# A prefix state through normed x, three token tiles, pre-tiled weights and a placed schedule, in a two-layer mLSTM and gMLP trunk on eight cores

## The chip, the cores and the metric

The kernel runs on all 8 cores of one Trainium2 chip: cores 0 to 3 are die 0, cores 4 to 7 are die 1. The metric is the device time of the slowest core, in microseconds. Each number of a profile below is of one execution, read on its slowest core.

The granted TensorE clock below is the share of its full clock that TensorE was allowed, as the profile records it. An execution of this program falls into one of two states. In the fast state all eight cores agree within about 1%. In the slow state the cores of one die (sometimes both) show a lower granted TensorE clock and the time is some per cent longer, whatever the kernel. Only fast runs are compared here, with fast runs. A ratio is the mean time of one kernel's fast runs over that of the kernel before's fast runs of the same rounds. So it is not quite the ratio of the medians that are quoted beside it.

## The reference

Input and output are (4 batches, 4096 tokens, 2048 channels) in f32. There are two layers, each with an RMS norm in front and a residual add behind, and a final norm. Cut to what matters:

```python
def mlstm_layer(xn, ...):                 # layer 0
    p = xn @ w_in                         # columns [q | k | v | o | z | gates]
    qk = silu(causal_depthwise_conv(p[..., :o1], conv_w, conv_b))   # 4 taps
    ...                                   # 8 heads: q, k 256 wide; v 512 wide
    hc = mlstm_cell(q * 256 ** -0.5, k, v, ig, lf)
    hc = hc * sigmoid(o); hc = hc * rsqrt(mean(hc * hc) + EPS) * head_g
    return (hc * silu(z)) @ w_out

def _mlstm_chunk(carry, inp):             # the cell, chunk by chunk
    ...
    h = num / max(|den|, exp(-m_t))
    c_new = decay * c_st + einsum('bhsd,bhse->bhde', k * wexp, v)   # state: 256 x 512 a head
    n_new = decay * n_st + einsum('bhs,bhsd->bhd', wexp, k)

def gmlp_layer(xn, ...):                  # layer 1
    p = xn @ w_in                         # [u | v | z], u and v through gelu
    sv = einsum('gts,bcsgd->bctgd', tril(w_s), layernorm(v)) + b_s   # within 128 tokens
    return (u * sv * silu(z)) @ w_out
```

## The kernel before

Core c takes batch c // 2 and half c % 2 of its tokens, 2048 of them. The second half of a sequence needs the cell's state at the end of the first half. So every core first computes that state from the first half's tokens (the "prefix") and multiplies it by a flag of 0 or 1. After that it runs both layers on its own tokens ("main"). Matmuls are bf16 with 512 columns at most. A weight tile is 2048 x 512, 2 MB as bf16; GpSimd's queue loads it and converts it from f32, into three slots in turn.

The prefix takes the 2048 tokens as four tiles of 512. For every head it projects k and v and updates the state once a chunk of 128 tokens:

```python
def state_update(h, c, cbi):
    for cc in range(2):
        tk.mm([lambda p, cc=cc: p.matmul(PK[cc][:, :], lhsT=kp[:, c, cc * 128:(cc + 1) * 128], rhs=vt[:, c, :],
                                         start=True, stop=True)], ...)
    ...
    for cc in range(2):
        tk.op("dve", lambda v, cc=cc: v.tensor_tensor(out=Cst[:, h, cc, :], in0=PK[cc][:, :], in1=Cst[:, h, cc, :],
                                                      op=ALU.add), ...)
    ...
    for cc in range(2):
        tk.op("act", lambda a, cc=cc: a.activation(out=Cst[:, h, cc, :], in_=Cst[:, h, cc, :], func=AF.Copy, scale=eg), ...)
```

Main takes four tiles of 512 tokens too. Each starts with a barrier and with the norm of its own x, which needs the x load, which needs the buffer of the previous tile's residual:

```python
for t in range(NT):
    tk.barrier()
    layer0(t)
    layer1(t)
    final_norm(t)          # ends with: ensure_gain(g0bc_d); load_x(xm, t + 1)
```

Weights are read from the original matrices, so a partition's share of a tile comes as 16 pieces of 2 KB in f32:

```python
w_in0v = w_in0.rearrange("(kc p) c -> p kc c", p=128)
def col_tile(wv, c0, n=512):
    return [(0, n, 0, KC, wv[:, :, c0:c0 + n])]
```

The softmax here doesn't subtract the row's maximum and nothing guards it: scores larger than these inputs give would overflow.

Of the kernel before, what the change touches and what calls it, by code (L numbers as in the profile page):

```python
# [6 lines left out]
F32 = mybir.dt.float32  # L7
BF16 = mybir.dt.bfloat16
AF = mybir.ActivationFunctionType
ALU = mybir.AluOpType  # L10

D = 2048
NTOK = 2048
T = 512
NSUB = T // 128
NT = NTOK // T
KC = D // 128
H = 8
EPS = 1e-6
IN0 = 16400  # L20
IN1 = 12288
SAME_ENGINE_SYNC = True
NWSLOT = 3

class Buf:
    __slots__ = ("w", "r", "name")

    def __init__(self, name=""):
        self.w = None
        self.r = {}  # L30
        self.name = name

# [5 lines left out]

class TK:
    def __init__(self, nc, es):  # L40
        self.nc = nc
        self.es = es
        self.eng = {"pe": nc.tensor, "act": nc.scalar, "dve": nc.vector,
                    "pool": nc.gpsimd, "sp": nc.sync}
        self.sem = {k: es.enter_context(nc.semaphore("s_" + k)) for k in self.eng}
        self.cnt = {k: 0 for k in self.eng}
        self.seen = {k: {} for k in self.eng}
        self.ndsem = 0

    def dsem(self):  # L50
        self.ndsem += 1
        key = "d%d" % self.ndsem
        return DSem(self.es.enter_context(self.nc.semaphore(key)), key)

    def wait(self, e, tk):
        if tk is None:
            return
        sem, val, key = tk
        if key == e and (e == "pe" or not SAME_ENGINE_SYNC):
            return  # L60
        if self.seen[e].get(key, 0) >= val:
            return
        self.eng[e].wait_ge(sem, val)
        self.seen[e][key] = val

    def _deps(self, e, reads, writes):
        for b in reads:
            self.wait(e, b.w)
        for b in writes:
            self.wait(e, b.w)  # L70
            for t in b.r.values():
                self.wait(e, t)
# [8 lines left out]
    def op(self, e, fn, reads=(), writes=()):  # L81
        self._deps(e, reads, writes)
# [4 lines left out]
        self._mark(tk, reads, writes)  # L87
        return tk

    def mm(self, fns, reads=(), writes=()):  # L90
        e = "pe"
        self._deps(e, reads, writes)
        ins = None
        for fn in fns:
            ins = fn(self.eng[e])
        self.cnt[e] += 1
        ins.then_inc(self.sem[e], 1)
        tk = (self.sem[e], self.cnt[e], e)
        self._mark(tk, reads, writes)
        return tk  # L100

    def dma(self, e, ds, out, in_, reads=(), writes=()):
        self._deps(e, reads, writes)
# [3 lines left out]
        self._mark(tk, reads, writes)  # L107
        return tk

    def snapshot(self):  # L110
        return [(self.sem[e], self.cnt[e], e) for e in ("pe", "act", "dve") if self.cnt[e] > 0]

    def barrier(self, engines=("pe", "act", "dve", "sp"), tks=None):
        if tks is None:
            tks = self.snapshot()
        for f in engines:
            for tk in tks:
                if tk[2] != f:
                    self.wait(f, tk)

class WQ:
    def __init__(self, tk, slots, tiles):
        self.tk = tk
        self.slots = slots
        self.tiles = tiles
        self.nl = 0
        self.nu = 0

    def _load(self):
        i = self.nl  # L130
        if i >= len(self.tiles):
            return
        t, b, ds = self.slots[i % len(self.slots)]
        tk = self.tk
        tk._deps("pool", (), [b])
        for (co, ncol, k0, nk, src) in self.tiles[i]:
            tk.eng["pool"].dma_start(out=t[:, k0:k0 + nk, co:co + ncol], in_=src).then_inc(ds.sem, 16)  # L137
            ds.cnt += 16
        tk._mark((ds.sem, ds.cnt, ds.key), (), [b])
        self.nl += 1  # L140

    def prime(self):
        for _ in self.slots:
            self._load()

    def cur(self):
        assert self.nu < len(self.tiles), "weight stream exhausted"
        t, b, ds = self.slots[self.nu % len(self.slots)]
        return t, b

    def peek(self, k):
        assert self.nu + k < self.nl, "tile not prefetched yet"
        t, b, ds = self.slots[(self.nu + k) % len(self.slots)]
        return t, b

    def done(self):
        self.nu += 1
        self._load()

def build_program():  # L160
    nc = bass.Bass("TRN2", target_bir_lowering=False)
    dt = lambda n, s, k="ExternalInput": nc.dram_tensor(n, s, F32, kind=k).ap()
    xm = dt("xm", [NTOK, D])
    xp = dt("xp", [NTOK, D])
    flag_d = dt("flag", [128, 1])
    w_in0 = dt("w_in0", [D, IN0])
    w_out0 = dt("w_out0", [4096, D])
    w_in1 = dt("w_in1", [D, IN1])
    w_out1 = dt("w_out1", [4096, D])
    g0bc_d = dt("g0bc", [128, D])  # L170
    g1bc_d = dt("g1bc", [128, D])
    gfbc_d = dt("gfbc", [128, D])
# [3 lines left out]
    hgbc_d = dt("hgbc", [128, 4096])  # L176
# [3 lines left out]
    bsbc_d = dt("bsbc", [128, 8 * 128])  # L180
# [3 lines left out]

    w_in0v = w_in0.rearrange("(kc p) c -> p kc c", p=128)
    w_in1v = w_in1.rearrange("(kc p) c -> p kc c", p=128)
    w_out0v = w_out0.rearrange("(kc p) c -> p kc c", p=128)
    w_out1v = w_out1.rearrange("(kc p) c -> p kc c", p=128)

    with ExitStack() as es:  # L190
        tk = TK(nc, es)
        sb = lambda n, s, d: es.enter_context(nc.sbuf_tensor("sb_" + n, s, d))
        ps = lambda n, s, d: es.enter_context(nc.psum_tensor("ps_" + n, s, d))

        Hs = sb("Hs", [128, NSUB, D], F32)
        Hb = [Buf("H%d" % i) for i in range(NSUB)]
        xnT = sb("xnT", [128, KC, T], BF16)
        xnTb = [Buf("xnT%d" % i) for i in range(NSUB)]
        YT = sb("YT", [128, 32, T], BF16)
        YTb = [Buf("YT%d" % i) for i in range(32)]  # L200
        Cst = sb("Cst", [128, H, 2, 512], F32)
        Cstb = [[Buf("C%d_%d" % (i, j)) for j in range(2)] for i in range(H)]
        nst = sb("nst", [128, H, 2], F32)
        nstb = [Buf("n%d" % i) for i in range(H)]
        wslots = []
        for i in range(NWSLOT):
            wslots.append((sb("w%d" % i, [128, KC, 512], BF16), Buf("w%d" % i), tk.dsem()))
        AB = sb("AB", [128, 12544], BF16)
        AFt = sb("AFt", [128, 1540], F32)
        xnb = AB[:, 6144:8192]  # L210
        xnbb = Buf("xnb")
        wg = sb("wg", [128, KC, 16], BF16); wgb = Buf()
        flag = sb("flagt", [128, 1], F32); flagb = Buf()
        convw = sb("convw", [128, 32, 4], F32); convwb = Buf()
        convb = sb("convb", [128, 32], F32); convbb = Buf()
        gateb = sb("gateb", [128, 16], F32); gatebb = Buf()
        lng = sb("lng", [128, 32], F32); lngb = Buf()
        lnb = sb("lnb", [128, 32], F32); lnbb = Buf()
        wsf = AFt[:, 0:1024].rearrange("p (g t) -> p g t", g=8); wsfb = Buf()
        wsm = sb("wsm", [128, 8, 128], BF16); wsmb = Buf()  # L220
        bsbc = sb("bsbc", [128, 8, 128], F32); bsbcb = Buf()
        rsbc = sb("rsbc", [128, 8, 128], F32); rsbcb = Buf()
        maskT = sb("maskT", [128, 128], F32); maskTb = Buf()
        identf = AFt[:, 1028:1156]; identfb = Buf()
        ident = sb("ident", [128, 128], BF16); identb = Buf()
        onesf = sb("onesf", [128, 128], F32); onesfb = Buf()
        onesb = sb("onesb", [128, 2], BF16); onesbb = Buf()
        hgh1 = sb("hgh", [128, 512], F32)
        hgh = [hgh1, hgh1]
        hghb1 = Buf()  # L230
        hghb = [hghb1, hghb1]
        hghs1 = tk.dsem()
        hghs = [hghs1, hghs1]
        halo = sb("halo", [128, 32, 4], F32); halob = [Buf() for _ in range(32)]
        gI = sb("gI", [128, NSUB, 8], F32); gIb = Buf()
        gZ = sb("gZ", [128, NSUB, 8], F32); gZb = Buf()
        gA = sb("gA", [128, NSUB, 8], F32); gAb = Buf()
        gL = sb("gL", [128, NSUB, 8], F32); gLb = Buf()
        beta = sb("beta", [128, NSUB, 8], F32); betab = Buf()
        beta16 = sb("beta16", [128, NSUB, 8], F32); beta16b = Buf()  # L240
        emb = sb("emb", [128, NSUB, 8], F32); embb = Buf()
        egt = sb("egt", [128, NSUB, 8], F32); egb = Buf()
        eg16t = sb("eg16t", [128, NSUB, 8], F32)
        sm = sb("sm", [128, 64], F32)
# [8 lines left out]
        def ab(o, n):  # L253
            return AB[:, o:o + n]
# [713 lines left out]
```

## Time and profile before

| reading | value | view |
|---|---|---|
| time, 3 runs | 5990, 6005 and 6534 us, the last slow | run times |
| TensorE busy | 5260.5 of 6024.2 us, 87% | page, part 1 |
| end of the prefix | 1190 us, TensorE busy 944 | stretches |
| rest | 4834 us, TensorE busy 4317 | stretches |
| TensorE idle at the start of a main tile | 45.5 to 47.9 us, three times | waits of those stretches |

The page of the kernel before, parts 1 to 4. Part 1 is busy time, its share and the number of instructions. Part 2 cuts the span into 40 slices, in tenths of busy time or of full clock. Part 3 is the DMA queues with packets, MB and their share of the 16 engines' time. Part 4 is the chain of work that ended last, by engine.

```profile
span 6024.2 us, 74749 instructions; the slowest of 8 cores (5953.9 to 6024.2 us)
PE 5260.5 (87%) x26660; PEld 2447.1 (41%) x26660; DVE 1937.1 (32%) x3333; ACT 2254.9 (37%) x4580; POOL 448.9 (7%) x397
...
PE   4988878788899996888899968888999778889998
...
PEclk8878887899999998999999989999999889999999
...
DMA packets 826206, 790.53 MB, mean 131 GB/s; under 512 B 10608, under 2 KB 813808, under 8 KB 818160
...
q0 software_dynamic: 811152, 713.12, 90.9%
...
PE 78%; DVE 7%; ACT 6%; issue 5%; DMA 3%; DVEq 0%; SPq 0%; ACTq 0%; another core or an unknown queue 0%; POOLq 0%
```

TensorE is the engine to look at: nothing else is half as busy, and it makes up 78% of the chain. The PE row dips to 6 or 7 at slices 16, 24 and 32, eight slices apart. Those are the starts of the second to fourth main tile.

The same kernel's stretches: the prefix and the rest. Columns are the stretch, its length, the busy time of each engine (with instructions), the granted clock, the DMA share and GB/s.

```profile
0.00:1190.20 1190.20, 943.60 (x4821) 435.37 (x4822) 431.86 (x722) 521.70 (x1069) 89.36 (x82) 0.84 0.94 118
1190.20:6024.20 4834.00, 4316.95 (x21845) 2011.78 (x21842) 1505.29 (x2611) 1733.25 (x3511) 359.51 (x315) 0.97 0.95 135
```

Its waits of TensorE. Each line says who waited (engine, tile, line), for whom, us in total, times and the longest.

```profile
PE ps_PT L422 <- DVE sb_AB L411: 154.3, 7, 47.9
PE ps_PS L694 <- DVE sb_sm L716: 136.8, 96, 1.8
PE ps_PT L739 <- DVE sb_AB L753: 101.6, 64, 2.1
PE ps_PT L422 <- ACT sb_AB L396: 46.9, 1, 46.9
...
PE ps_PJ L443 <- DMA sb_w<-w_in: 4.0, 1, 4.0
PE ps_PJ L457 <- DMA sb_w<-w_out: 3.0, 2, 1.8
```

A wait of 47.9 us once is another thing than 96 waits of 1.8 us: the first is a hole, the second a chain that is a little too long for its slot. Weight DMA, with 91% of the engines' time on its queue, costs TensorE 8 us in all (4.0 + 3.0 and a line of 1.0 left out). So weights, busy as their queue was, were no limit here.

The hole itself, in the timeline of the kernel before at the start of its second main tile. Columns are start, length, engine, instruction, count, and in brackets the engine's idle time before and what ended it.

```profile
2332.09 7.07 PE L457 MATMUL ps_PS<-sb_w,sb_YT 128*128 128x512 bf16 x32
...
2360.11 6.95 SPq L104 DMA_DIRECT2D sb_Hs<-xm  x4
...
2381.54 1.91 ACT L396 ACTIVATE sb_AB<-sb_Hs 128x2048 bf16<-128x2048 f32 x1 [21.63 <-DMA sb_Hs<-xm]
...
2387.07 1.01 PE L422 MATMUL ps_PT<-sb_ident,sb_AB 128*128 128x128 bf16 x8 [47.91 <-DVE sb_AB L411]
```

The last matmul of one tile ends at 2339.2 us. The final norm then runs, x is asked for at 2360, arrives 21 us later, is squared, scaled and transposed, and TensorE starts again at 2387.

The floor under all this, the time that the matmuls alone would take, is read from one piece of the chain of the kernel before, in order of time (start, length, what):

```profile
1894.98 103.60 PE ps_PJ L452 x480
```

480 matmuls of 512 columns back to back took 103.60 us, 215.8 ns each. The Trainium skill, "TensorE: Matmul & The Clock Gate", section "Wait — 56ns, not 53.3ns?", gives columns / 2.4 ns plus about 2.5 ns, so 215.8; the trace agrees.

### The profile page before, as it was taken

The page shows a single profiled execution, that of the slowest core. Times are in us where ns is not written, and L with a number is a line of the kernel's source. Part 1 is how long each engine was busy: PE and PEld are TensorE (multiplying, and loading weights), DVE is VectorE, ACT ScalarE, POOL GpSimd, SP SyncE. Part 2 cuts the span into 40 slices and gives each one's busy share as a digit, 9 for nine tenths or more (in the row PEclk, how much of TensorE's full clock was granted, in tenths as well). Part 3 has the DMA queues.
Part 4 walks back from the last instruction along what each step waited for, and adds up shares of the span by engine and source line. Part 5 has one row for each costly group of instructions (what it writes and reads, how often), then busy time and mean ns, then how long its engine had stood idle before and what let it go on. Part 6 is the DMA issues. An engine that isn't in the chain of part 4 may idle for free.

```text
span 6024.2 us, 74749 instructions; the slowest of 8 cores (5953.9 to 6024.2 us)
## 1 busy us (share of the span) xinstructions
PE 5260.5 (87%) x26660; PEld 2447.1 (41%) x26660; DVE 1937.1 (32%) x3333; ACT 2254.9 (37%) x4580; POOL 448.9 (7%) x397
## 2 busy tenths in 40 slices
PE   4988878788899996888899968888999778889998
PEld 2434433334444443344444433444444334444443
DVE  2334332333331331334312313333124133341132
ACT  3445443454532321444423214544132045541320
POOL 0000000000000000000000000000000000000000
PEclk8878887899999998999999989999999889999999
DMA  8989899989999999799999996988999979999997
GB/s 137 106 115 119 113 135 108 108 104 120 123 136 143 150 148 162 101 121 125 127 146 150 150 165 102 125 120 127 147 150 151 145 126 122 121 125 146 151 150 127
DMA packets 826206, 790.53 MB, mean 131 GB/s; under 512 B 10608, under 2 KB 813808, under 8 KB 818160
## 3 DMA queue, kind: packets, MB, share of 16 engines
q0 software_dynamic: 811152, 713.12, 90.9%
q1 hardware_dynamic: 14688, 72.61, 3.6%
q8 instruction: 219, 3.59, 0.2%
q14 instruction: 147, 1.20, 0.1%
HBM read 1482.02 MB, written 16.78 MB: 249 GB/s over the span
## 4 chain that ended last, share of the span: by engine, by line
PE 78%; DVE 7%; ACT 6%; issue 5%; DMA 3%; DVEq 0%; SPq 0%; ACTq 0%; another core or an unknown queue 0%; POOLq 0%
PE ps_PJ L452 32%; PE ps_PJ L443 25%; PE ps_PJ L457 7%; PE ps_PS L457 4%; PE ps_PN L457 4%; DVE sb_Cst L544 2%; DVE sb_AFt L516 2%; PE ps_PK L535 1%; DMA sb_Hs<-xm 1%; DVE sb_AB L753 1%; ACT L729 1%; ACT L747 1%; ACT sb_AB L747 1%; ACT sb_AB L396 1%; DMA sb_w<-w_out 1%
## 5 line engine op out<-in xcount | busy, mean ns | idle before, releaser
L452 PE MATMUL ps_PJ<-sb_w,sb_xnT 128*128 128x512 bf16 x9984 | 2292.4, 387 | 60.9 <-ACT sb_AFt L506 25.0
L443 PE MATMUL ps_PJ<-sb_xnT,sb_w 128*128 128x512 bf16 (+1 forms) x7424 | 1645.0, 380 | 19.9 <-ACT sb_AFt L508 14.5
L452 PEld LDWEIGHTS ps_PJ<-sb_w,sb_xnT 128*128 128x128 bf16 x9984 | 974.9, 99 | 1218.0 <-issue 225.5
L443 PEld LDWEIGHTS ps_PJ<-sb_xnT,sb_w 128*128 128x128 bf16 x7424 | 711.3, 100 | 869.3 <-issue 136.8
L137 POOL DMA_DIRECT2D sb_w<-w_in x328 | 374.3, 1142 | 4641.8 <-PE ps_PJ L443 1325.3
L544 DVE TENSOR_TENSOR sb_Cst<-ps_PK,sb_Cst 128x512 f32<-128x512 f32 x512 | 330.8, 687 | 827.8 <-PE ps_PK L535 492.4
L457 PE MATMUL ps_PJ<-sb_w,sb_YT 128*128 128x512 bf16 x2048 | 451.6, 379 | 3.0 <-DMA sb_w<-w_out 3.0
L516 DVE SCALAR_TENSOR_TENSOR sb_AFt<-sb_AFt,sb_convw 128x512 f32<-128x512 f32 x576 | 432.6, 751 | 61.2 <-DVE sb_AFt L516 0.9
L557 ACT ACTIVATE sb_Cst<-sb_Cst,sb_egt 128x512 f32<-128x512 f32 x512 | 340.1, 711 | 69.0 <-DVE sb_Cst L544 63.0
L520 ACT ACTIVATE sb_AB<-sb_AFt 128x512 bf16<-128x512 f32 x192 | 120.8, 629 | 543.5 <-DVE sb_AFt L516 419.2
L457 PEld LDWEIGHTS ps_PJ<-sb_w,sb_YT 128*128 128x128 bf16 x2048 | 199.8, 98 | 243.5 <-issue 4.4
L396 ACT ACTIVATE sb_AB<-sb_Hs 128x2048 bf16<-128x2048 f32 x48 | 91.3, 1902 | 529.4 <-DVE sb_sm L391 439.2
L512 DVE TENSOR_SCALAR sb_AFt<-sb_AFt,sb_convw,sb_convb 128x512 f32<-128x512 f32 x192 | 105.3, 549 | 562.4 <-ACT sb_AFt L508 562.4
L858 DVE SCALAR_TENSOR_TENSOR sb_AFt<-ps_PD,sb_lng,sb_bsbc 128x512 f32<-128x512 f32 x128 | 96.1, 750 | 466.4 <-PE ps_PD L855 466.3
L535 PE MATMUL ps_PK<-sb_AB 128*128 128x512 bf16 x512 | 177.5, 407 | 68.3 <-DVE sb_Cst L544 42.7
L422 PE MATMUL ps_PT<-sb_ident,sb_AB 128*128 128x128 bf16 x192 | 19.5, 263 | 241.3 <-DVE sb_AB L411 154.3
L457 PE MATMUL ps_PN<-sb_w,sb_YT 128*128 128x512 bf16 x1024 | 230.2, 379 | 0.0
L457 PE MATMUL ps_PS<-sb_w,sb_YT 128*128 128x512 bf16 x1024 | 230.2, 379 | 0.0
L769 DVE TENSOR_TENSOR sb_Hs<-ps_PJ,sb_Hs 128x512 f32<-128x512 f32 x64 | 44.2, 691 | 563.0 <-PE ps_PJ L457 563.0
L882 ACT ACTIVATE sb_AB<-sb_Hs 128x2048 bf16<-128x2048 f32 x16 | 30.5, 1909 | 446.7 <-DVE sb_sm L880 445.6
L508 ACT ACTIVATE sb_AFt<-ps_PJ 128x512 f32<-128x512 f32 x192 | 114.6, 597 | 198.8 <-PE ps_PJ L443 187.1
L694 PE MATMUL ps_PS<-sb_AB 128*128 128x128 bf16 x256 | 35.7, 222 | 158.6 <-DVE sb_sm L716 136.8
(152 smaller groups left out, 3918.9 us busy)
## 6 DMA issues: line engine op xcount, KB each, us to landing
sb_w<-w_in POOLq DMA_DIRECT2D x224, 2048.0 KB, 18.5
sb_w<-w_out POOLq DMA_DIRECT2D x64, 2048.0 KB, 16.1
sb_w<-w_in POOLq DMA_DIRECT2D x104, 1024.0 KB, 18.7
sb_Hs<-xp SPq DMA_DIRECT2D x16, 1024.0 KB, 6.9
sb_Hs<-xm SPq DMA_DIRECT2D x16, 1024.0 KB, 22.7
out<-sb_YT SPq DMA_DIRECT2D x16, 1024.0 KB, 29.3
sb_hgh<-hgbc SPq DMA_DIRECT2D x32, 256.0 KB, 4.3
sb_AB<-g0bc SPq DMA_DIRECT2D x4, 1024.0 KB, 16.5
```

The costliest lines, as they stand in the source:

```text
L137: tk.eng["pool"].dma_start(out=t[:, k0:k0 + nk, co:co + ncol], in_=src).then_inc(ds.sem, 16)
L396: tk.op("act", lambda a: a.activation(out=junkN, in_=Hs[:, s, :], func=AF.Square, accum_out=sm[:, s:s + 1]), reads=[Hb[s]], writes=[junkNb ...
L443: tk.mm([lambda p, kc=kc: p.matmul(pj[:, 0:n], lhsT=wt[:, kc, c0:c0 + 128], rhs=xnT[:, kc, t0:t0 + n], start=(kc == 0), stop=(kc == KC - 1 ...
L452: fns = [lambda p, kc=kc: p.matmul(pj[:, 0:n], lhsT=xnT[:, kc, s * 128:(s + 1) * 128], rhs=wt[:, kc, 0:n], start=(start and kc == 0), stop ...
L457: fns = [lambda p, kc=kc: p.matmul(pj[:, 0:n], lhsT=lhs(kc), rhs=wt[:, kc, 0:n], start=(start and kc == 0), stop=(stop and kc == kcs - 1)) ...
L508: tk.op("act", lambda a: a.activation(out=cbuf[:, 3:3 + T], in_=pj[:, 0:T], func=AF.Copy), reads=[pjb], writes=[cbufb])
L516: tk.op("dve", lambda v, j=j: v.scalar_tensor_tensor(out=acc, in0=cbuf[:, j:j + T], scalar=convw[:, ch, j:j + 1], in1=acc, op0=ALU.mult, o ...
L520: tk.op("act", lambda a: a.activation(out=dstT[:, cc, :], in_=acc, func=AF.Silu), reads=[accb], writes=[dstb])
L535: tk.mm([lambda p, cc=cc: p.matmul(PK[cc][:, :], lhsT=kp[:, c, cc * 128:(cc + 1) * 128], rhs=vt[:, c, :], start=True, stop=True)], reads=[ ...
L544: tk.op("dve", lambda v, cc=cc: v.tensor_tensor(out=Cst[:, h, cc, :], in0=PK[cc][:, :], in1=Cst[:, h, cc, :], op=ALU.add), reads=[PKb[cc]] ...
L557: tk.op("act", lambda a, cc=cc: a.activation(out=Cst[:, h, cc, :], in_=Cst[:, h, cc, :], func=AF.Copy, scale=eg), reads=[egb], writes=[Cst ...
L747: tk.op("act", lambda a, c=c, pj=pj: a.activation(out=sz[:, c, :], in_=pj[:, :], func=AF.Silu), reads=[pjb], writes=[szb])
```

## The change

The intent has five parts.

1. Prefix state in another order. With v = xn Wv, the state at the end of the prefix is the sum over tokens of w k v, which equals (sum over tokens of w k xn) Wv. The sum over tokens costs 1024 matmuls and the product with Wv 256. In exchange go the v projection of the prefix (2048) and the per-chunk state updates (256). All decays are known once the gates are, so there is no chunk-to-chunk recurrence. The normed x is stored to DRAM while it is made and reloaded, 1 MB at a time, as the stationary operand of the sums.
2. Three main tiles of 6, 5 and 5 chunks of 128 tokens instead of four of 4. Each weight is read three times instead of four.
3. Weights are laid out in tiles in DRAM before the launch, so that each partition reads its share of a tile as one contiguous row of 32 KB.
4. A schedule list: projection groups of 16 matmuls are slots, and the steps of the cell, the norm and the output are hung on slots. The norm of the next tile runs inside the output projection of this one.
5. Small things: the convolution reads PSUM directly, the state's decay and add are one VectorE instruction, and the inverse root of the norms is made on GpSimd.

The diff, cut to its core (lines are cut inside as well, where "..." stands, and the comments are added):

```diff
-T = 512
-NT = NTOK // T
+MAIN = [6, 5, 5]
+PRE = 16
...
-        def state_update(h, c, cbi):                 # once a chunk and head, prefix and main
...
+        def gpair(hp, jp, k):                        # prefix: sum over chunks of (normed x) x (weighted k)
+            if k == 0:
+                if jp == 0:
+                    xload(0)
+                    xload(1)
+                elif jp + 1 < 8:
+                    xload(jp + 1)
...
+                mm([XSb[i]] + KPb, [pjb], [(pj[:, :], XSt[:, i, c, k * 128:(k + 1) * 128], KP[:, c, :], c == 0, c == P - 1)
+                                           for c in range(P)])
+        def cgrp(hp, hh, cc, wi):                    # prefix: times the v weights, to DRAM
+            mm([wb] + GTb, [pkb], [(pk[:, :], GT[:, j, ...], w[:, j, :], j == 0, j == 15) for j in range(16)])
+            dve([pkb, flagb], [cstgb[cc]], "tensor_scalar", out=cstg[:, cc, :], in0=pk[:, :], scalar1=flag[:, 0:1], ...)
+            dma("sp", css[cc], cst_d[h][:, cc * 512:(cc + 1) * 512], cstg[:, cc, :], R=[cstgb[cc]], W=[])
...
+        for c in range(P + 3):                       # prefix: stages of the norm
+            st = []
+            if c < P:
+                st.append((na, c))                   # load x, square, inverse root
+            if 0 <= c - 1 < P:
+                st.append((nb_, c - 1))              # scale, store the normed x
+            if 0 <= c - 2 < P:
+                st.append((nc_, c - 2))              # transpose
...
-            tk.eng["pool"].dma_start(out=t[:, k0:k0 + nk, co:co + ncol], in_=src).then_inc(ds.sem, 16)
+        dma("pool", ds, w[:].rearrange("p k c -> p (k c)"), wt_d[tiles[i]], W=[b])
...
+            for c in range(n):                       # main: steps of the cell hung on v and z groups
+                S.at(b + 2 * c, lambda c=c: s_step(h, c))
+                i0 = b + 2 * c + 1
+                S.at(i0, lambda c=c: c_step(h, c))
+                i1 = max(i0 + 2, zid[c] + 1)
+                S.at(i1, lambda c=c: y1_step(h, c))
+                S.at(i1 + 1, lambda c=c: y2_step(h, c))
...
-        for t in range(NT):
-            tk.barrier()
+        if t + 1 < len(MAIN):                        # norm of the next tile inside this one's output projection
+            ie = norm_tile(t + 1, 0, lastl1 + 3, 3, STG, [(PT, PTb), (PS, PSb)])
...
+    return w[:, cols].reshape(KC, 128, 512).transpose(1, 0, 2).reshape(128, KC * 512)
```

## The prediction

> **What bounds it now.** TensorE: busy 5260.5 of 6024.2 us (87%), and 78% of the chain that ended last. The matmul floor, worked out from durations in the chain of waits: 480 back-to-back 512-column matmuls take 103.60 us, 215.8 ns each. That agrees with the Trainium skill, "TensorE: Matmul & The Clock Gate", section "Wait — 56ns, not 53.3ns?" (columns/2.4 ns plus 2.5 ns). About 22,400 of these, 2,560 128-column ones (56 ns in the timeline) and small ones make about 5040 us; the other 960 us is TensorE idle or slowed. From the stretches by stage: the prefix (to about 1190 us) has a floor of about 770, so it loses 420, its granted clock being 0.77 to 0.90; each main tile takes about 1218 us for a floor of 1067, a loss of 140 to 150: 45 to 48 us at each tile start (transposes waiting for the norm), the clock dip after it, and cell waits (over all tiles 137 us before the score matmuls, 102 us before the y transposes). Weight DMA is not the limit: TensorE waits about 8 us for it.
>
> **What the change does.**
> - TensorE work: the prefix v projection (2048 matmuls) and state updates (256) go; (k times normed x) costs 1024 and the product with v weights 256. Saves 1024 x 216 ns = 221 us. Main columns stay the same. New floor about 4810 us (prefix 543, main 4265).
> - Prefix structure: no per-chunk recurrence, no tile barriers. I expect 650 to 750 us instead of 1190: floor 543 plus about 75 us start, about 50 us where ScalarE waits in order for x loads during the first k groups, about 35 us for gates and first transposes, some clock dips.
> - Main: three tiles (6, 5, 5 chunks) instead of four, norms of the next tile hidden in output-projection groups, so the 45 us holes go; cell steps are spread over v and z groups, two groups (6.9 us) per chunk against a state chain I estimate at about 5 us. I expect about 100 us lost, against 570.
> - Weights: 228 tiles of 2 MB instead of about 340, demand 100 to 120 GB/s against 150 sustained now. Worth little.
> - VectorE: the state decay merges into one operation. Convolution now reads PSUM directly: 3 x about 0.62 us per 384 columns against 2.6 us of TensorE; small stalls with the previous head's y steps.
>
> **Sum.** 4810 + about 190 (prefix) + about 100 (main) = about 5100 us, ratio about 0.85. 80% range 4920 to 5380. Faster by over 2%: 0.97; within: 0.02; slower: 0.01.
>
> **What would show it.** TensorE busy share 94% or more; prefix ending at 650 to 750 us; no idle gap over 10 us at tile starts; granted clock 0.97 or more after the prefix; VectorE under 50%; weight-DMA waits under 50 us in total; GB/s about 110 to 120.
>
> **What would make it wrong.** (a) Denser TensorE work on all cores lowers the granted clock: the skill page (section "Seeing it yourself") tells of a 13/16 limit for dense all-core matmuls, but this trace shows 1.00 for hundreds of us at 100% busy, so unlikely; if it held, about 5700. (b) PSUM-reading convolution makes VectorE the limit in query/key groups. (c) x or x-transposed reloads (1 MB per 6.9 us of TensorE) stall the k-times-x groups. (d) Strict order on ScalarE makes the prefix's x loads cost more than 50 us.

## The result, and the profile after

The changed kernel took 5240, 5242 and 5262 us in its fast runs (two more were slow, 5417 and 5591). The ratio to the kernel before is 0.875, interval 0.872 to 0.878. The outputs agree with the reference, though part of the prefix is computed from wrong data (see "The order of the norm stages").

| | before | after | difference |
|---|---|---|---|
| span of the profiled core | 6024.2 | 5240.7 | -783.5 |
| prefix | 1190.2 | 829.2 | -361.0 |
| of that TensorE busy / idle | 943.6 / 246.6 | 602.6 / 226.6 | -341.0 / -20.0 |
| main | 4834.0 | 4411.5 | -422.5 |
| of that TensorE busy / idle | 4317.0 / 517.0 | 4282.9 / 128.6 | -34.1 / -388.4 |

Idle is length less busy. The two halves of the gain are of different kinds. The prefix got shorter because TensorE has less to do there; its idle time hardly changed. Main got shorter because TensorE waits less; its work hardly changed. Of the 341 us in the prefix, 221 is work removed by the count of matmuls. The other 120 goes with matmuls that ran less slowed: the granted clock rose from 0.84 to 0.92. The Trainium skill, "TensorE: Matmul & The Clock Gate", section "What's actually happening", says that the array is throttled by default and that activity releases it. The trace fits that (1.00 between 3000 and 3200 us with TensorE 99% busy, 0.92 in the prefix with its many gaps), but no run here tested it, so the cause of these 120 us is not shown. The number of matmuls rose, from 26,660 to 28,660, although the work fell: groups of 384 columns make more and shorter ones.

The page of the changed kernel, the same parts as before:

```profile
span 5240.7 us, 75792 instructions; the slowest of 8 cores (5203.3 to 5240.7 us)
PE 4885.4 (93%) x28660; PEld 2620.4 (50%) x28660; DVE 1712.7 (33%) x3188; ACT 1674.6 (32%) x3161; POOL 320.9 (6%) x629
...
PE   2888779999999999989899999999889999999999
...
PEclk9899889999999999999999999999999999999999
...
DMA packets 84678, 637.48 MB, mean 122 GB/s; under 512 B 8416, under 2 KB 25312, under 8 KB 43744
...
q0 software_dynamic: 32976, 478.23, 49.8%
...
PE 87%; DMA 8%; DVE 2%; ACT 1%; issue 1%; SPq 0%; POOL 0%; DVEq 0%; ACTq 0%; POOLq 0%
```

The PE row now is weak in its first six slices, the prefix, and nearly even after them. The weight queue moves its bytes in 32,976 packets instead of 811,152, and takes half of the engines' time instead of 91%. But the chain has 8% DMA in it, where there was 3%.

The changed kernel's stretches:

```profile
0.00:829.20 829.20, 602.56 (x3788) 320.94 (x3789) 273.24 (x423) 227.67 (x354) 45.19 (x63) 0.92 0.47 120
829.20:5240.70 4411.50, 4282.86 (x24873) 2299.49 (x24871) 1439.47 (x2765) 1446.97 (x2807) 275.75 (x566) 0.99 0.61 122
```

The changed kernel's waits of TensorE:

```profile
PE ps_PJ L159 <- DMA sb_xst<-xsd: 54.5, 3, 20.4
PE ps_PT L157 <- ACT sb_pn_121 L143: 52.3, 7, 31.3
PE ps_PK L159 <- DVE sb_pxT L610: 51.2, 1, 51.2
PE ps_PJ L159 <- ACT sb_so L143: 38.6, 2, 20.9
PE ps_PT L157 <- DVE sb_ybf L146: 37.1, 21, 2.0
PE ps_PT L157 <- ACT sb_pn_122 L143: 22.6, 7, 3.6
PE ps_PT L157 <- DVE sb_xnb_84 L146: 22.4, 3, 7.9
PE ps_PK L157 <- DVE sb_cstg L146: 20.8, 9, 8.7
PE ps_PT L157 <- DVE sb_xnb_83 L146: 14.1, 2, 8.7
```

Here is what the old entries became. The 47.9-us holes for the norm are now waits of at most 8.7 us (the two lines of the normed x, sb_xnb, 36.5 us together). The 137 us before the score matmuls (query times key of a chunk) are gone from the list. The 102 us before the y transposes (the cell's output y, turned for the output projection) are 37. Weight waits are none. New are: the reload of the normed x (sb_xst, 54.5), the transposes of the prefix waiting on ScalarE's squares (sb_pn, 74.9), the start (51.2), the store of the prefix states (sb_cstg, 20.8), and two holes of some 20 us that carry the name of the output gate (sb_so).

Two of these lines name the wrong culprit, and the order of time shows the right one. The chain of the changed kernel at the second of its main tiles, some of the pieces up to the restart of TensorE:

```profile
2469.80 22.71 DMA out<-sb_H
...
2493.78 31.74 DMA sb_C<-cst
...
2526.81 0.49 ACT sb_so L143
...
2527.44 5.80 PE ps_PJ L159 x16
```

TensorE waited for a bank that ScalarE was to empty (sb_so). In ScalarE's program the copy of the first head's state stands in front of that, and the state (256 KB a transfer, sb_C) took 31.7 us to load. Its load stood in SyncE's queue behind the load of the head's gain (a scale for each channel of the cell's output), which shares a place in SBUF with a row block of the previous tile's output and so waited for the store of that block; the store took 22.7 us where the median of its kind is 4.5. So the chain under "sb_so" is two slow small transfers. That they follow one another is not what makes it long: "The state load before the gain load" below takes the store out of the state's way, and the state lands only 4 us earlier.

And the start of the changed kernel, the longest piece of its chain before 60 us:

```profile
6.41 41.99 DMA sb_idf<-ident
```

The identity, 64 KB, took 42.0 us to land. In the kernel before the same load took 16.5 us.

### The profile page after: what moved, and what is told of

Its sections match the earlier page's. It is cut to its first block, busy times and chain, and to the rows that moved or that the text cites. A ratio compares the mean times of both kernels' runs of the same rounds, so it can differ in the third digit from the quotient of the medians.

```text
span 5240.7 us, 75792 instructions; the slowest of 8 cores (5203.3 to 5240.7 us)
## 1 busy us (share of the span) xinstructions
PE 4885.4 (93%) x28660; PEld 2620.4 (50%) x28660; DVE 1712.7 (33%) x3188; ACT 1674.6 (32%) x3161; POOL 320.9 (6%) x629
## 3 DMA queue, kind: packets, MB, share of 16 engines
q0 software_dynamic: 32976, 478.23, 49.8%
## 4 chain that ended last, share of the span: by engine, by line
PE 87%; DMA 8%; DVE 2%; ACT 1%; issue 1%; SPq 0%; POOL 0%; DVEq 0%; ACTq 0%; POOLq 0%
PE ps_PJ L159 73%; PE ps_PK L159 6%; PE ps_PN L159 5%; DMA sb_xs_77<-xm 2%; PE ps_PT L157 1%; DMA cst<-sb_cstg 1%; DMA out<-sb_H 1%; DMA sb_C<-cst 1%; DMA sb_xst<-xsd 1%; PE ps_PS L159 1%; DMA sb_idf<-ident 1%; DVE sb_acc L146 1%; DMA sb_px_119<-xp 0%; DMA sb_px_120<-xp 0%; DVE sb_hc L146 0%
## 5 line engine op out<-in xcount | busy, mean ns | idle before, releaser
L159 PE MATMUL ps_PJ<-sb_w_73,sb_xnT 128*128 128x512 bf16 x2816 | 630.2, 381 | 38.6 <-ACT sb_so L143 38.6
L159 PE MATMUL ps_PJ<-sb_w_72,sb_xnT 128*128 128x512 bf16 x2816 | 626.0, 379 | 0.0
L159 PE MATMUL ps_PJ<-sb_w_71,sb_xnT 128*128 128x512 bf16 x2560 | 570.6, 379 | 0.0
L159 PE MATMUL ps_PJ<-sb_xnT,sb_w_71 128*128 128x384 bf16 (+3 forms) x3456 | 520.9, 310 | 5.0 <-DVE sb_acc L146 5.0
L159 PE MATMUL ps_PJ<-sb_xnT,sb_w_72 128*128 128x384 bf16 (+3 forms) x3072 | 465.2, 310 | 0.0
L159 PEld LDWEIGHTS ps_PJ<-sb_w_73,sb_xnT 128*128 128x128 bf16 x2816 | 274.2, 98 | 359.8 <-issue 45.2
L159 PEld LDWEIGHTS ps_PJ<-sb_w_72,sb_xnT 128*128 128x128 bf16 x2816 | 272.8, 98 | 315.4
L159 PEld LDWEIGHTS ps_PJ<-sb_xnT,sb_w_71 128*128 128x128 bf16 x3456 | 334.9, 98 | 165.8 <-issue 6.2
L159 PE MATMUL ps_PJ<-sb_xnT,sb_w_73 128*128 128x384 bf16 (+3 forms) x2688 | 402.6, 309 | 0.0
L159 PEld LDWEIGHTS ps_PJ<-sb_w_71,sb_xnT 128*128 128x128 bf16 x2560 | 248.1, 98 | 286.8
L146 DVE SCALAR_TENSOR_TENSOR sb_acc<-ps_PJ,sb_convw,sb_acc 128x384 f32<-128x384 f32 (+1 forms) x576 | 324.9, 572 | 175.7 <-ACT sb_acc L143 133.7
L159 PEld LDWEIGHTS ps_PJ<-sb_xnT,sb_w_72 128*128 128x128 bf16 x3072 | 297.1, 98 | 140.8 <-issue 1.5
L159 PEld LDWEIGHTS ps_PJ<-sb_xnT,sb_w_73 128*128 128x128 bf16 x2688 | 260.1, 98 | 122.9
L159 PE MATMUL ps_PJ<-sb_kpp,sb_xst 128*128 128x512 bf16 x1024 | 229.3, 386 | 54.5 <-DMA sb_xst<-xsd 54.5
L143 ACT ACTIVATE sb_Cb<-sb_C 128x512 bf16<-128x512 f32 (+1 forms) x232 | 156.2, 673 | 235.7 <-DVE sb_C L146 170.3
L146 DVE SCALAR_TENSOR_TENSOR sb_pacc<-ps_PJ,sb_convw,sb_pacc 128x410 f32<-128x410 f32 (+1 forms) x240 | 154.9, 645 | 125.8 <-ACT sb_pacc L143 106.3
L143 ACT ACTIVATE sb_acc<-ps_PJ,sb_convb,sb_convw 128x384 f32<-128x384 f32 x192 | 122.0, 636 | 224.8 <-PE ps_PJ L159 224.3
L159 PE MATMUL ps_PJ<-sb_w_73,sb_YT 128*128 128x512 bf16 x864 | 192.4, 379 | 0.0
L146 DVE TENSOR_TENSOR sb_H<-ps_PJ,sb_H 128x512 f32<-128x512 f32 x72 | 49.8, 692 | 435.2 <-PE ps_PJ L159 435.2
```

Of the source, the lines that this page charges most:

```text
L143: return self.op("act", lambda a: a.activation(**k), R, W)
L146: return self.op("dve", lambda v: getattr(v, m)(**k), R, W)
L159: ins = p.matmul(o[0], lhsT=o[1], rhs=o[2], start=o[3], stop=o[4])
```

## The experiments

All twelve kernels of these runs gave outputs that agree with the reference. They ran in three batches, each on one chip, beside runs of the kernel before. So ratios are compared where there are any; where there is none, microseconds are set against the 5240.7 us of the changed kernel's profiled run. The kernel before took 5964 to 6020 us in the fast runs of the three batches and 5990 to 6015 beside the changed kernel, so some 30 us between batches mean little by themselves. Comments in the diffs are added for the reader.

The open questions were these. The prefix took 829 us where 733 were predicted (a floor of 543 and a loss of 190), main 4411 where 4365 were. One theory blamed the arrangement in the prefix and the tile starts: buffers too few, loads too late. The rival blamed the new weight rows: transfers of 32 KB pieces crowd out the small loads beside them. Other runs test terms of the prediction alone.

### Weights in 16 pieces of 2 KB, and in 4 of 8 KB

The tiles keep their place in DRAM; only the length of the contiguous pieces changes (16 pieces for u_rows2k, 4 for v_rows8k).

```diff
-    wt_d = dt("wt", [NTILE, 128, KC * 512])
+    wt_d = dt("wt", [NTILE, 16, 128, KC * 512 // 16])
-        dma("pool", ds, w[:].rearrange("p k c -> p (k c)"), wt_d[tiles[i]], W=[b])
+        dma("pool", ds, w[:].rearrange("p (g k) c -> p g (k c)", g=16), wt_d[tiles[i]].rearrange("g p c -> p g c"), W=[b])
```

> Undoes the long weight rows alone: the same weight tile is fetched as 16 pieces of 2 KB per partition, as before, instead of one of 32 KB. Theory A (rows are worth little, as predicted): time within 0.7% of the changed kernel (5205 to 5275 us), weight transfers from 14.3 back to about 16 to 18 us from issue to landing, mean DMA busy share from about 0.55 to about 0.8. Rival B (the long rows make the short side loads wait, so the other queue's loads are what cost the 140 us over the prediction): with short weight rows the identity constant lands after about 17 us instead of 42, x tiles of the next token tile after under 10 instead of 13.3, the state load at the tile start after under 15 instead of 32, TensorE waits at those places drop by at least half, and the kernel gets faster by 30 us or more. Rival C (long rows are a real gain): slower by over 1.5%.

> The same tile as 4 pieces of 8 KB per partition. A: within 0.7% of the changed kernel. B: between the two, side loads land sooner than with 32 KB rows, so faster than the changed kernel by 15 us or more. C: like the changed kernel, within 0.5%.

Measured: with 2 KB 0.867 (0.865 to 0.869), with 8 KB 0.862 (0.860 to 0.863); the changed kernel has 0.875 (0.872 to 0.878). Shorter pieces made the kernel faster, by 0.9% and 1.5% (0.8668 / 0.875 and 0.8617 / 0.875). The chain lines of the same identity load, first with 2 KB:

```profile
6.16 11.71 DMA sb_idf<-ident
```

then with 8 KB, followed by what is left of the hole at the tile start in the waits of that run:

```profile
6.84 27.50 DMA sb_idf<-ident
...
PE ps_PJ L159 <- ACT sb_so L143: 2.3, 1, 2.3
```

The identity took 42.0, 27.5 and 11.7 us for pieces of 32, 8 and 2 KB. By itself that gained little: the first sums over chunks came at 311, 305 and 303 us. The wait for the stores of prefix states fell from 20.8 to 6.2 us in both. The hole at the tile start fell from 38.6 us to 2.3 with 8 KB and left the list with 2 KB: in the 8-KB run the same store of output rows took 11.7 us, not 22.7, so that the state load was issued that much earlier, and the four state loads there took 23.2 us (median), not 31.6. With the norms at the tile starts (18.7 us instead of 36.5), that is most of what main gained, 4346 instead of 4411 us; the prefix ended at 799 instead of 829. The price of 2 KB: weights wait again, here in its waits of TensorE, and the queue takes 66.6% of the engines' time instead of 49.8%.

```profile
PE ps_PJ L159 <- DMA sb_w<-wt: 26.5, 5, 9.9
```

So crowding is real, and the piece length has a middle. The Trainium skill, "DMA: Bandwidth & Descriptors", section "Queues, rings and completion order", says that each DMA engine goes round the queue rows that have work, and changes row only at packet boundaries. The counts fit that: going from 1 piece to 4 a row added 87,552 packets, which is 3 for each of the 228 tiles x 128 rows. So the profile counts a piece as one packet. Worked out from the share of the weight queue and its packets, a packet took an engine about 0.12 us with 2 KB, 0.35 with 8 KB and 1.27 with 32 KB, an estimate. That the wait at packet boundaries is the cause is an inference from this fit; that the piece length is the cause is shown.

### Four tiles again

```diff
-MAIN = [6, 5, 5]
+MAIN = [4, 4, 4, 4]
```

> Undoes the three token tiles alone: four tiles of 4 chunks. TensorE columns stay equal; weights read once more (292 tiles instead of 228), one more tile start. The prediction's view (tile count matters only by the holes at the starts): each start still costs about 40 to 45 us of TensorE idle time (norm of the next tile 22, state load 18 to 21), so about 45 us for the extra start plus 8 heads and 8 spatial groups of about 2 us: 5300 to 5350 us. Rival (with the same weight demand per matmul as before, 2 MB per 13.8 us, the transfers become the limit): TensorE waits for weights of over 50 us in total, over 5400 us.

Measured: 0.911 (0.904 to 0.917), fast runs 5417 to 5463 us. The tile count is worth 4%, where the expectation had about half of that; this was a miss. The time is the rival's (over 5400 us), but not its sign: TensorE waited for weights only 10.5 us, not over 50. The prefix stayed (828 us), main grew from 4411 to 4591: 129 us of it are idle, 50 are busy time (28,013 matmuls instead of 24,873, narrower ones). The waits say where the idle time is: the y transposes 66.4 us instead of 37.1, the norms 58.5 instead of 36.5, the state loads at three tile starts 52.8 instead of 38.6 at two, the convolution 24.7 instead of 5.0, and waits for residual rows of 29.1 (16.7 and 12.4) that were not there. So a tile costs its start and its thinner heads. The traffic of its weights may cost too, through the loads beside it: the residual rows took 35.3 us (median) to land instead of 18.0, with 65.3% instead of 49.8% of the engines' time on the weight queue. No run separates the two.

### The chunks of the cell one group apart

The score and state step of a chunk goes to every projection group instead of every second one.

```diff
-                S.at(b + 2 * c, lambda c=c: s_step(h, c))
-                i0 = b + 2 * c + 1
+                S.at(b + c, lambda c=c: s_step(h, c))
+                i0 = b + c + 1
```

> Undoes the two-group spacing of the cell steps alone: one chunk step per projection group (3.45 us) instead of one per two groups (6.9 us), all else equal. If the state chain takes about 5 us as estimated, TensorE waits about 1.5 us or more per chunk, 128 chunk steps, so about 150 to 250 us slower (5400 to 5490 us), with the waits on the score or state matmuls released by VectorE or ScalarE. Rival (the chain is hidden by the buffers anyway and the spacing is worth nothing): within 1% of 5241 us.

Measured: 0.884 (0.882 to 0.886), so 1% longer, where 3 to 5% were expected; the alternative, within 1% of 5241 us, is what came (5277 and 5282). A miss, and it corrects a term of the prediction: the chain from one chunk's state matmul to the next scaled state was estimated at 5 us. In the trace it takes 3.7 us (from 899.5 to 903.2 in the changed kernel). A slot of one group is 3.45 us of projection plus 1.2 us of the step's own matmuls (0.10, 0.67 and 0.43 in the chain), 4.65 us, so the chain still fits. Main grew by 40 us: 17 are idle, most of them at the y transposes (49.8 instead of 37.1 us), and 23 are TensorE busy for longer, with a granted clock of 0.98 instead of 0.99. Two groups a chunk had more room than was needed.

### The removed work put back

The sums over chunks are computed twice into the same bank, 1024 more matmuls, the number that the new order saves. The first group of each pair of heads is written apart in the code and is doubled too.

```diff
-                                           for c in range(P)])
+                                           for _twice in range(2) for c in range(P)])
```

> Puts the saved matmuls back: each of the 64 groups of k-times-x matmuls runs twice into the same bank (1024 extra 512-column matmuls, results unchanged). If the matmuls saved by the new prefix count in full on the time, as the prediction takes it: 221 us more than the changed kernel, 210 to 230 us, all of it in the prefix. Rival (the k-times-x phase is paced by the transfers of the normed x, 1 MB per 6.9 us, so TensorE work is not what counts there): under 170 us more, with the 54 us of waits on those transfers gone.

Measured: 0.910 (0.904 to 0.916). The profiled span is 5459.2 us, 218.5 more than the changed kernel's; the prefix ended at 1049 instead of 829 us. 1024 x 215.8 ns is 221. So the saved matmuls count in full: the G groups (the sums over chunks) lie on the critical path, nothing hides under them. The waits for the reloaded x stayed:

```profile
PE ps_PJ L159 <- DMA sb_xst<-xsd: 55.4, 3, 21.3
```

So they do not come from a lack of bandwidth during the G groups; as they did not shrink with twice the time to load in, they should sit at the start of a pair of heads, where the next run looks.

### Room in the prefix: four staging buffers, earlier reloads

The store of a prefix state had two staging buffers, and the reload of x for the next pair of heads was issued when its first group was due.

```diff
-        cstg = mem.at("cstg", [2, 512], F32, A4 + 3584)
+        cstg = mem.at("cstg", [4, 512], F32, A4 + 3584)
...
                 if jp == 0:
-                    xload(0)
-                    xload(1)
+                    if hp == 0:
+                        xload(0)
+                        xload(1)
                 elif jp + 1 < 8:
                     xload(jp + 1)
+                elif hp < 3:
+                    xload(0)                 # for the next pair; its second half likewise, one group later
```

> Takes the waits between the prefix's last step for one head pair and the first for the next away: four staging buffers for the states on their way out instead of two, and the first two loads of normed x for the next pair issued before that step rather than after its stores. Nothing else changed (32 KB weight rows). If the loads' place in the queue is what costs the 54 us (waits of TensorE on the normed x, 17 to 20 us three times) plus about 21 us on the staging buffers and a clock dip of some us each: 60 to 90 us faster than the changed kernel. Rival (the loads are slow because the long weight rows crowd them out, wherever they stand): under 30 us faster, the waits stay.

Measured: 0.865 (0.858 to 0.872), the profiled run 52 us shorter than the changed kernel's (expected 60 to 90). The prefix ended at 779 us instead of 829, main did not move. Waits for x went from 54.5 to 26.3 us and those for the staging buffer from 20.8 to 6.1. So the arrangement matters as well. The staging wait is one that the shorter rows cured too: two causes, the slow store and the few buffers, and either cure suffices.

### An earlier start

x is loaded three chunks ahead, only one weight tile is asked for at first, and the store of a table needed much later no longer stands in front of the x loads.

```diff
-        dma("sp", tk.dsem(), rs_d, rsf[:], R=[rsfb], W=[rs_b])
+        rs_sem.append(tk.dsem())             # the store itself moves to the end of the k groups
...
+            nl(0)
+            nl(1)
             load_G(dr["g0_d"])
+            nl(2)
...
-    for _ in range(3):
-        wload()
+    wload()
```

> Changes the start alone: x tiles and gain are issued ahead, the store of the row sums no longer stands in front of them in the queue, three x buffers loaded two stages ahead instead of two, and only one weight tile is requested at once, the other two after the first and fourth norm. If the start (first k group at 109 us, k groups until 290 us, of which 112 us is matmul time) waits for those loads: first k group before 80 us, k groups done before 235 us, 45 to 75 us faster than the changed kernel. Rival (VectorE and ScalarE, not the loads, pace the first k groups): first group earlier by about 30 us, but the k groups still take 160 us or more, so 25 to 35 us faster.

Measured: 0.871 (0.858 to 0.883), two fast runs at 5206 and 5242 us: nothing to 36 us where 45 to 75 were expected. A miss. On the profiled core the first matmul came at 26 us instead of 51, the first k group (projection to keys) at 93 instead of 109, but the first G group only at 305 instead of 311, and the prefix ended at 836 instead of 829. The waits of the transposes on ScalarE's squares stayed, 81.7 us against 74.9; the next run shows what they are. The rest is the clock: on six of the eight cores the prefix ended at 785 to 805 us, where the cores of the changed kernel have 812 to 829. Cores 0 and 1, of which core 1 decides the time, had a granted clock of 0.81 between 92 and 280 us, the six others 0.84 to 0.88, and ended at 822 and 836. So the earlier start gains some 25 us (mean of the six) where the clock is not lower, close to the 25 to 35 of the expectation's alternative; why the clock was lower on two is open.

### The order of the norm stages

In the changed kernel the timeline around 86 us reads as follows (sb_px holds x, sb_pn the normed x in two buffers, 121 and 122):

```profile
75.87 2.35 DVE L146 SCALAR_TENSOR_TENSOR sb_pn_122<-sb_px_120,sb_sm,sb_G 128x2048 bf16<-128x2048 f32 x1 [0.97 <-POOL sb_sm L149]
...
84.07 1.91 ACT L143 ACTIVATE sb_pn_121<-sb_px_119 128x2048 bf16<-128x2048 f32 x1 [10.58 <-DMA sb_px_119<-xp]
...
86.21 1.01 PE L157 MATMUL ps_PT<-sb_ident,sb_pn_121 128*128 128x128 bf16 x8 [31.26 <-ACT sb_pn_121 L143]
...
88.19 2.35 DVE L146 SCALAR_TENSOR_TENSOR sb_pn_121<-sb_px_119,sb_sm,sb_G 128x2048 bf16<-128x2048 f32 x1 [9.96 <-PE ps_PN L157]
```

The squaring (84.07) needs only its sum; its elements are thrown away, into the buffer of the chunk's normed x. But stages run in the order: square chunk c, scale chunk c-1, transpose chunk c-2, and chunks c and c-2 share a buffer. So the transposes at 86.21 wait 31 us for the x load of a chunk two later. Worse, what they read is what the squaring wrote: VectorE's scaling of buffer 121 comes only at 88.19. For prefix chunks 0 to 13 the changed kernel transposes squares instead of the normed x, so k and the gates of these chunks are wrong. All variants of the changed kernel run here share this fault, except f_order, best2 and best2_4k.

The outputs still agree. An argument for that, not tested: the forget-gate bias of the reference is about 3, a factor of sigmoid(3) = 0.953 a token, and chunks 0 to 13 end at least 256 tokens before the main half, which leaves 0.953 to the power 256, about 4e-6. A comparison with other gate biases would show the fault. The kernel's own dependency tracking cannot: it orders the accesses as the program states them.

The repair is to transpose first:

```diff
-            if c < P:
-                st.append((na, c))
-            if 0 <= c - 1 < P:
-                st.append((nb_, c - 1))
             if 0 <= c - 2 < P:
                 st.append((nc_, c - 2))
+            if c < P:
+                st.append((na, c))
+            if 0 <= c - 1 < P:
+                st.append((nb_, c - 1))
```

> One swap in the prefix, on the changed kernel (32 KB rows): in each stage the transposes of chunk c come before the squaring of chunk c+2, which writes its throw-away output over the same buffer. In the changed kernel the order is the other way round, so the transposes of the first 14 prefix chunks read squares, not the normed x (the outputs pass all the same), and TensorE waits for that squaring: 75 us in 14 waits. Theory: with the swap the waits named after that squaring go from 75 to under 45 us (the first ones still wait for the x loads), the k groups end 25 us or more earlier, and the kernel gets 25 to 45 us faster, still correct. Rival (the loads of x pace it, the squaring is only the last to come): under 10 us.

Measured: fast runs 5181 and 5183 us, the profiled run 59 us shorter than the changed kernel's, where 25 to 45 were expected (no ratio: too few fast runs in common rounds). Beside f_cload (below), which ran in the same batch and is as slow as the changed kernel, it is 50 us. The first G group came at 258 instead of 311 us, and the prefix ended at 755 to 784 us on the eight cores instead of 812 to 829. In the waits of this run the transposes no longer wait for ScalarE's squares but three times for VectorE's scaling:

```profile
PE ps_PT L157 <- DVE sb_pn L146: 31.3, 3, 20.0
```

So 44 of 75 us of these waits came from an order that nothing in the mathematics asked for.

### The state load before the gain load

At the start of a main tile, the first head's state is loaded ahead of the head's gain, not behind.

```diff
-            hgload(0)
             cload_(0)
+            hgload(0)
```

> One swap at a tile start, on the changed kernel (32 KB rows): the load of the state goes ahead of the gain load in the queue; the gain's place overlaps the last output rows, the state's does not. Theory 1 (queue order): the two stalls of TensorE at a tile start released by ScalarE's output-gate evacuation (39 us together) fall below 12 us, 25 to 35 us faster. Theory 2 (the long weight rows crowd out the state's short rows, wherever it stands in the queue): the state load still takes over 20 us and over 25 us of the stalls stay.

Measured: 0.876 (0.873 to 0.880), 5232 us, the same as the changed kernel. The holes under "sb_so" stayed at 36.2 us. The chain of this run has the state load as follows:

```profile
2472.22 49.13 DMA sb_C<-cst
```

It went out 22 us earlier (2472.2 instead of 2493.8), before the store had landed, and still landed only at 2521.4 instead of 2525.5. So the order of the two loads in the queue is not the cause, as the second theory expected; with the weight rows of 8 KB the same holes were 2.3 us, so the long weight rows are.

### All repairs together

best1 joins the 8-KB rows, the prefix room, the earlier start and the swapped loads with two edits that were not run alone: a second buffer for the next tile's x, loaded one step earlier, and the y transposes one group later.

```diff
-                S.at(i1 + 1, lambda c=c: y2_step(h, c))
+                S.at(i1 + 2, lambda c=c: y2_step(h, c))
...
-            S.at(i, a0)
+            S.at(max(i - step, i0), a0)
```

> All together: 8 KB weight rows, both prefix changes, two x buffers for the norms of the next token tile, the state load ahead of the gain load at a tile start, y transposes one group later. If the waits are separate and add up: about 95 (rows) + 75 (queue order) + 45 to 60 (start, partly in the rows' 95 already) + 37 (y transposes) + 15: 4980 to 5040 us, ratio to before 0.835 to 0.845, TensorE idle under 170 us. Rival (the waits give way to one another, or a denser TensorE loses granted clock): above 5080 us.

Measured: two fast runs at 5029 and 5030 us, as expected (no ratio: too few fast runs in common rounds). The prefix took 752 us, main 4275. The norms at the tile starts and the y transposes are gone from the list of waits; 82.5 us of what is left are the transposes waiting for the squares. This kernel still has the faulty order.

best2 adds the repaired order, an own buffer for the squares and a third buffer for the normed x, and asks for the second and third weight tile later:

```diff
-            norm_a(px[c % 3][:], [pxb[c % 3]], pn[c % 2][:], pnb[c % 2], sl[c])
+            norm_a(px[c % 3][:], [pxb[c % 3]], pjk[:], pjkb, sl[c])
```

> The last combination plus the swapped order, a buffer of its own for the squares, three buffers for the normed x of the prefix, second and third weight tile asked for later: 40 to 70 us below the last combination's 5029 us, so 4960 to 4990 us, ratio to before 0.83; TensorE idle under 130 us. If VectorE and ScalarE pace the first k groups, under 20 us gained.

> The same with 8 weight pieces of 4 KB per partition instead of 4 of 8 KB. If shorter weight rows go on helping the side loads: 5 to 20 us faster than with 8 KB; if the weights' own rate is what counts by now: within 5 us, or slower by waits for weights (26 us of them were seen with 2 KB pieces).

Measured: best2 0.832 (0.829 to 0.836), fast runs 4967 and 4972 us, within the 4960 to 4990 expected; with 8 pieces of 4 KB instead of 4 of 8 KB (best2_4k) 0.833 (0.831 to 0.836), 4973 to 4977 us. The two piece lengths do not differ. The page and the stretches of best2:

```profile
span 4970.8 us, 75826 instructions; the slowest of 8 cores (4958.1 to 4970.8 us)
PE 4845.5 (97%) x28660; PEld 2606.2 (52%) x28660; DVE 1705.7 (34%) x3188; ACT 1670.6 (34%) x3161; POOL 362.9 (7%) x629
```

```profile
0.00:693.00 693.00, 584.82 (x3788) 313.62 (x3789) 272.15 (x423) 226.68 (x354) 32.55 (x63) 0.93 0.59 144
693.00:4970.80 4277.80, 4260.70 (x24873) 2292.60 (x24871) 1433.59 (x2765) 1443.95 (x2807) 330.31 (x566) 1.00 0.66 126
```

TensorE is busy 97% of the time, the same number of matmuls as in the changed kernel. Main lost 17 us to idle, against 129; the prefix lost 108, against 227. best2 beats both kernels: it is 5% faster than the changed one (0.8324 / 0.875 = 0.951), and it transposes the right data.

## Why the prediction was right or wrong

The time was predicted as 5100 us with a range of 4920 to 5380; measured were 5240, 5242 and 5262 in the fast runs. Direction and size held: 0.875 where about 0.85 was named.

Right, and shown:

- TensorE bounds the kernel, and 221 us of its work go away. Putting 1024 matmuls back cost 218.5 us.
- The 45-us holes for the norm at tile starts go. The largest such wait is now 8.7 us. That is read from the waits of the two kernels; no run put the norms back.
- The granted clock stays: 0.99 after the prefix. The worry (a), the limit of 13/16 for dense matmuls on all cores, did not come true in the fast runs.
- VectorE is at 33% (under 50% named) and DMA at 122 GB/s (110 to 120 named, so just above); weights cost no wait (under 50 us named). The worry (b), convolution on PSUM, cost 5.0 us of waits.

Wrong in size, by term of the sum:

- "Prefix ... 650 to 750 us", in the sum a floor of 4810 "+ about 190 (prefix)". It was 829 us, a loss of 286. Three terms failed. "About 75 us start" was 109 us to the first k group, with an identity that took 42 us to land while the first weight rows were loading; asking for less at first (f_start) made that 93. "About 50 us where ScalarE waits in order for x loads", the worry (d), came as 75 us of transposes waiting for the squares; most of that was a false order through a shared buffer, which the reading of the code had missed (swapping it gave 50 to 59 us). The worry (c), reloads of x stalling the G groups, cost 54.5 us, and the stores of states 20.8; the sum had nothing for either. Main idea and floor were right: best2, with the same matmuls, ends its prefix at 693.
- "+ about 100 (main)". It was 146 us (4411.5 less the floor of 4265). The tile starts kept 38.6 us of state loads, 36.5 of norm waits, and the y transposes 37.1. So "no idle gap over 10 us at tile starts" failed twice, with a new cause: two slow small transfers, crowded by the weight rows.
- "Weights ... Worth little". The new rows were worth less than nothing: with the same tiles in pieces of 8 KB the kernel is 1.5% faster, of 2 KB 0.9%. The prediction counted bytes and the weight queue's own waits, both of which came out as said, and not what a long piece does to the others' transfers.
- "Two groups ... against a state chain I estimate at about 5 us". The chain is 3.7 us; the estimate was on the safe side and cost nothing.
- "TensorE busy share 94% or more". It was 93%, which is these two losses seen again.

The sum of the miss: 5240.7 is 141 over the predicted 5100, of which the prefix is 96 (829 against 733) and main 46 (4411 against 4365), rounded.

What stays open: the two edits of best1 that were never run alone (second buffer for x, later y transposes) share 71 us of main (4346 with 8-KB rows alone, 4275 in best1) with the earlier start and swapped loads, and were not told apart. The 120 us of the prefix that go with the granted clock were not told from the removed work by a run. Of the 388 us of idle time that main lost, runs tested only the tile count and the spacing of the cell steps; the rest is assigned by the lists of waits. And why some runs are slow was not looked into.

## What to carry to other kernels

When a linear projection feeds only a sum, take the sum first and project after: here that took 1024 matmuls off the critical path, and every one of them counted. Choose the piece length of a bulk stream by what it does to the small transfers beside it, not by its own rate; and when a stall bears the name of one engine, follow it back in time before believing the name. A throw-away output still occupies a buffer: give it one of its own, or it creates an order that nobody wants and can overwrite what is still to be read.

## What the Trainium skill lacked or had wrong

- "DMA: Bandwidth & Descriptors", section "Rules for kernel authors", tells to use at least 1 MiB a DMA, and nothing of what the length of pieces inside it does to other transfers. (Its nearest is in section "SWDGE vs HWDGE vs iDMA", which prefers a packet of at most 4096 B.) All weight loads here were 2 MB; cutting the 32-KB rows to 8 KB made the kernel 1.5% faster. A 64-KB load beside them landed in 27.5 instead of 42.0 us, and in 11.7 with 2-KB pieces; the holes at the tile starts fell from 38.6 to 2.3 us.
- The same page, section "Queues, rings and completion order", gives a packet as 9 to 17 descriptors as a rule. The profile's packets are something else or the loads here are another case: it counts one packet for each contiguous piece, 32,976, 120,528 and 470,736 on the weight queue for 1, 4 and 16 pieces a row. No run shows at which boundaries an engine changes rows.
- "TensorE: Matmul & The Clock Gate", section "Seeing it yourself", tells to budget 13/16 of the clock for dense matmuls on all cores on the default power profile, held while the load lasts (which profile this chip has is not on record). In the fast runs here the granted clock was 0.98 to 1.00 on all eight cores at once in a stretch of 200 us with TensorE 97 to 100% busy (both kernels). In one slow run of the four-tile kernel (6258 us) the mean clock was 0.80 to 0.81 on die 1, near 13/16, and 0.96 to 0.97 on die 0. Other slow runs have a slow die anywhere between 0.80 and 0.97, so these figures do not show that it is this limit.
- No page has a duration for a power on GpSimd, which the changed kernel uses for its inverse roots: 0.57 us for a 128x1 tile in the timeline, behind 0.22 us for the add before it. Nothing waited for it long enough to appear among TensorE's waits.
